# Attention's division put behind the second product, with its reciprocals sent through DRAM as rows, in a two-layer encoder

## The chip, the cores and the metric

The kernel runs on one core of one Trainium2 chip. The metric is the device time of one execution in microseconds; of several runs the median is used. One execution was also recorded by the profiler, and all rows of profile in this document come from such recordings. Engines are named as the profile names them: PE is the tensor engine's matmul unit, PEld its weight load, DVE the vector engine, ACT the scalar engine, POOL the GpSimd engine, SP the engine that issues most transfers.

## The reference

Two transformer layers over 1024 tokens of width 1024, in float32. Layer 0 has two groups of eight heads: A, grouped-query attention with rotary positions, and B, latent attention. Both are dense: every query sees all 1024 keys. Layer 1 has 16 heads that see keys within 128 tokens, with a distance penalty and a learned sink. In all three the output of a head is divided by its sum of exponentials and multiplied by a gate:

```python
# layer 0, group A (B likewise)
p = jax.nn.softmax(sc, axis=-1).astype(v.dtype)
o = jnp.einsum('bkgqs,bskd->bqkgd', p, v)
oa = oa * jax.nn.silu(ga)
# layer 1
p = jnp.exp(sc - m)
denom = jnp.sum(p, axis=-1, keepdims=True) + jnp.exp(sink_l - m)
o = jnp.einsum('bnkgqs,bnskd->bnqkgd', (p / denom).astype(v.dtype), vb)
return (oc * jax.nn.silu(gc)) @ w_out
```

Softmax is the exponentials over their sum. Since the second product (with `v`) is linear, dividing a query's exponentials by their sum gives the same as dividing that query's row of the output, or as dividing its row of the gate.

## The kernel before, in words

Each float32 matrix is split into a high and a low part, and a product is made of two or three matmuls of such parts. Matmuls have 128 x 128 weights and up to 512 columns.

**Layer 0's attention** runs in 32 steps (`run_groups`): head by head, each with two halves of 512 queries. A step makes four score tiles of 128 queries by 1024 keys (`softmax_unit`): PE makes the scores in PSUM, DVE finds each row's maximum (`nm`), ACT makes the exponentials into a tile of SBUF (`Pa` or `Pb` in the profile) and sums them on the way (`sm`), DVE takes the reciprocal (`rs`), and POOL multiplies the tile of 128 x 1024 by it, in place. In the same step PE makes the second product of the step before (`pv_step`): it transposes four 128 x 128 pieces into PSUM, ACT and DVE split them into high and low (`hla`, `hlb`), and two matmuls with `V` add up. In group B two of the eight pieces are split by POOL instead (`pv_ahead`). At the end ACT and DVE move the sum to `og`, 64 partitions for an even head and 64 for an odd one, and POOL multiplies it by the gate (`pv_final`). Two heads share a tile of `og`, which goes to DRAM when both are done (`spill`). Beside this, PE gets matmuls for the gates (`g_step`), and for what group B needs, in the steps of group A.

**Layer 1's attention** runs in 32 steps too: four key heads by eight blocks of 128 queries. `win_S` makes four score tiles of up to 384 keys, DVE adds the penalty, POOL puts the sink into a column behind them, ACT makes the exponentials, DVE takes four reciprocals at once (`dn`), and POOL multiplies each of the four tiles. `win_PV` does the transposes, splits and second product. For three of the four key heads the gate is made after the attention and multiplied into its output `og1` (`g_ft`); for the last the gates (`g1`) are made late and multiplied at the very end (after line 2730). Feature matmuls (`f_step`) fill PE between the steps, with weights that are loaded two tiles ahead and split by POOL (`f_load`).

After each attention comes the output projection (`wino_out`), as seven products of combined blocks, and after layer 1 a last normalisation.

**What sets the order.** No instruction is issued where the code names it. `Recorder` collects all of them; `run` (line 730) plays them through a model of the engines with estimated durations, priorities and limits on buffers, and so puts them into one order. `PLACES` (line 81) then moves single instructions: a pair (i, j) puts i right behind j. `emit` (line 1009) issues the result, so every instruction bears its line 1017 in the profile, and groups are told apart by their tiles. Each engine works through its own instructions in that order, and SP its transfers. `BANKS` gives each PSUM tile its bank. `UA_BUFS` and `SM_BUFS` are the numbers of half tiles (128 x 512) and of small tiles (128 x 16), `RESERVE` what the model keeps free of them.

Of the kernel before, what the change touches and what calls it, by code (L numbers as in the profile page):

```python
# [19 lines left out]
P = 128  # L20
# [20 lines left out]
UA_BUFS = 3  # L41
SM_BUFS = 32
# [3 lines left out]
RESERVE = {"u": 0, "PSUM": 0, "ua": 2, "sm": 11, "SP": 8}  # L46
# [9 lines left out]
AHEAD = {"a": {}, "b": {4: 0, 7: 3}}  # L56
# [983 lines left out]
def encoder_kernel(ctx: ExitStack, tc: tile.TileContext, xt, ada_t, w_c1, w_c2, w_c3, w_g0, w_uq, w_ukv, w_out0, w_v1,  # L1040
# [759 lines left out]

    def softmax_unit(qk, name):
        S = PS(f"S{name}")
        first = None
        for b in range(2):
# [8 lines left out]
        with rec.at(shift=PRIO["exp"]):  # L1815
            nc.scalar.activation(pt, S, AF.Exp, bias=nm[:, 0:1], accum_out=sm[:, 0:1])
# [900 lines left out]
    for g in range(4):  # L2717
        og1[g] = [U(f"og1{g}{half}") for half in range(2)]
        for i in range(NT):
            m0 = m_  # L2720
            if prev is not None:
                m_ = win_PV(*prev)
# [104 lines left out]
```

## Time and profile before

| what | value |
|---|---|
| median of 3 runs | 1132.57 us (1127.54 to 1133.49) |
| profiled execution | 1134.05 us, its span 1132.2 us, mean granted clock 0.985 |
| PE busy | 1102.4 us, 97% of the span |
| DVE, ACT, POOL busy | 978.1, 749.5, 745.3 us |
| layer 0's attention | about 140 to 640 us of the span |
| layer 1's attention | about 770 to 1037 us |

The span runs from the first to the last instruction. A group's row in the profile has the line, the engine, the operation, output and inputs, shapes and count; then busy time and the mean of one in ns; then the engine's idle time just before them, with what ended it. A row of waits has the waiting engine and tile, what it waited for, the total in us, how often, and the longest. A row of the timeline has the start and the length in us. A matmul's end is modelled by the profiler, so a busy PE can still be slower than it could be. The granted clock says at what share of full speed PE was allowed to run.

### The profile page before, as it was taken

What the parts mean: (1) busy time and instruction counts of PE and PEld (TensorE: products, weight loads), DVE (VectorE), ACT (ScalarE), POOL (GpSimd) and SP (SyncE); (2) the same over time, 40 slices, a digit from 0 to 9 for tenths busy, and PEclk for the clock granted to TensorE, in tenths of its full rate; (3) what the DMA queues carried; (4) which work ended last, traced back from release to release, by engine and by line L of the source; (5) the groups of instructions that cost most, each with busy time, mean ns of one, the idle gap of its engine ahead of it and who ended that gap; (6) DMA issues with size and microseconds to landing.
All of it is one profiled execution on the core that took longest, in us unless ns stands there. A gap on an engine that the chain in (4) does not pass through costs nothing.

```text
span 1132.2 us, 17617 instructions
## 1 busy us (share of the span) xinstructions
PE 1102.4 (97%) x5928; PEld 942.9 (83%) x5928; DVE 978.1 (86%) x1604; ACT 749.5 (66%) x1460; POOL 745.3 (66%) x732
## 2 busy tenths in 40 slices
PE   8999999999999999999999999999999999999996
PEld 7898877888887988888888877888888888888785
DVE  5978998898999988887888999998877787778995
ACT  4663554778777877887798742667776776766722
POOL 1135777988986737877879736757675775976422
PEclk7999999999999999999999999999999999999997
DMA  9869863564751486974785477401111221349303
GB/s 368 326 201 318 273 252 78 144 195 125 203 165 15 89 289 207 212 204 160 210 238 191 114 271 245 152 1 38 41 54 56 78 68 42 113 166 336 103 1 149
DMA packets 60026, 183.72 MB, mean 162 GB/s; under 512 B 7200, under 2 KB 9632, under 8 KB 58912
## 3 DMA queue, kind: packets, MB, share of 16 engines
q1 hardware_dynamic: 54464, 159.00, 40.2%
q0 software_dynamic: 4608, 22.02, 10.7%
q10 hardware_dynamic: 864, 1.57, 0.4%
q8 instruction: 47, 0.77, 0.3%
q14 instruction: 43, 0.35, 0.1%
HBM read 147.31 MB, written 70.91 MB: 193 GB/s over the span
## 4 chain that ended last, share of the span: by engine, by line
PE 81%; DVE 12%; issue 2%; ACT 2%; POOL 1%; DMA 1%; POOLq 0%; SPq 0%; DVEq 0%; ACTq 0%
PE psum L1017 81%; DVE nm L1017 1%; DVE xr L1017 1%; DVE hla L1017 1%; DVE t30l L1017 1%; DMA xT<-in_xt 1%; ACT Pb L1017 1%; DVE o L1017 0%; DVE T6l L1017 0%; DVE hlb L1017 0%; DVE s31l L1017 0%; DVE s30l L1017 0%; DVE psum L1017 0%; POOL sq L1017 0%; DVE t40l L1017 0%
## 5 line engine op out<-in xcount | busy, mean ns | idle before, releaser
L1017 DVE TENSOR_REDUCE nm<-psum 128x1 f32<-128x1024 f32 x128 | 155.6, 1219 | 21.0 <-PE psum L1017 18.8
L1017 POOL TENSOR_SCALAR Pa<-Pa,rs 128x1024 f32<-128x1024 f32 x64 | 77.4, 1233 | 34.9 <-DVE rs L1017 30.4
L1017 POOL TENSOR_SCALAR Pb<-Pb,rs 128x1024 f32<-128x1024 f32 x64 | 77.3, 1217 | 32.7 <-DVE rs L1017 29.7
L1017 POOL TENSOR_SCALAR p<-p,dn 128x384 f32<-128x384 f32 (+1 forms) x128 | 69.4, 560 | 33.2 <-DVE dn L1017 32.9
L1017 ACT ACTIVATE Pa<-psum,nm 128x1024 f32<-128x1024 f32 x64 | 71.6, 1119 | 27.6 <-DVE nm L1017 26.0
L1017 DVE TENSOR_TENSOR hla<-psum,hla 128x512 fp32r<-128x512 f32 x128 | 82.6, 683 | 4.4 <-ACT hla L1017 4.2
L1017 ACT ACTIVATE Pb<-psum,nm 128x1024 f32<-128x1024 f32 x64 | 71.9, 1124 | 20.2 <-DVE nm L1017 18.0
L1017 DVE CUSTOM_DVE_ANT_0 p<-psum,relt,sinkn 128x384 f32<-128x384 f32 (+1 forms) x128 | 70.4, 579 | 15.3 <-PE psum L1017 13.8
L1017 PE MATMUL psum<-hla,VA 128*128 128x512 f32 x256 | 80.5, 407 | 1.3 <-DVE og('0', 2)_631 L1017 1.1
L1017 ACT ACTIVATE p<-p,nm 128x385 f32<-128x385 f32 (+1 forms) x128 | 74.8, 591 | 10.2 <-DVE nm L1017 5.6
L1017 ACT CAST hla<-psum 128x512 fp32r<-128x512 f32 x128 | 70.5, 596 | 16.3 <-PE psum L1017 15.3
L1017 PE MATMUL psum<-k,q 128*128 128x512 f32 x256 | 80.5, 401 | 0.6 <-ACT Pb L1017 0.6
L1017 PE MATMUL psum<-hlb,VB 128*128 128x512 f32 x256 | 78.3, 409 | 0.5 <-DVE hlb L1017 0.5
L1017 PE MATMUL psum<-ident,Pa 128*128 128x128 f32 x512 | 73.4, 274 | 0.0
L1017 ACT CAST hl<-psum 128x512 fp32r<-128x512 f32 x88 | 48.7, 590 | 34.2 <-PE psum L1017 30.2
L1017 DVE TENSOR_TENSOR hlb<-psum,hlb 128x512 fp32r<-128x512 f32 x96 | 63.2, 684 | 8.7 <-ACT hlb L1017 8.2
L1017 PE MATMUL psum<-ident,Pb 128*128 128x128 f32 x512 | 70.3, 273 | 0.1
L1017 DVE TENSOR_TENSOR hl<-psum,hl 128x512 fp32r<-128x512 f32 x88 | 57.9, 686 | 12.9 <-ACT hl L1017 10.9
L1017 PEld LDWEIGHTS psum<-ident,Pa 128*128 128x128 f32 x512 | 61.4, 141 | 8.4 <-issue 0.2
L1017 PEld LDWEIGHTS psum<-ident,Pb 128*128 128x128 f32 x512 | 60.3, 140 | 9.0 <-ACT Pb L1017 0.5
L1017 ACT COPY ot<-psum 64x512 f32<-64x512 f32 x64 | 37.4, 584 | 39.6 <-PE psum L1017 38.5
L1017 ACT ACTIVATE sq<-xr 128x512 f32<-128x512 f32 (+2 forms) x30 | 19.3, 658 | 61.3 <-DVE xr L1017 61.3
(1152 smaller groups left out, 3845.3 us busy)
## 6 DMA issues: line engine op xcount, KB each, us to landing
ada<-in_ada_t SPq DMA_DIRECT2D x32, 512.0 KB, 8.1
fs<-in_w_f POOLq DMA_DIRECT2D x12, 768.0 KB, 9.2
adag<-in_ada_t SPq DMA_DIRECT2D x16, 512.0 KB, 5.3
ws<-in_w_out POOLq DMA_DIRECT2D x16, 512.0 KB, 6.5
S<-ws SPq DMA_DIRECT2D x16, 512.0 KB, 4.5
A<-in_w_out SPq DMA_DIRECT2D x12, 512.0 KB, 4.5
o<-spill SPq DMA_DIRECT2D x12, 512.0 KB, 5.5
fs<-in_w_f SPq DMA_DIRECT2D x6, 768.0 KB, 8.9
```

The costliest lines, as they stand in the source:

```text
L1017: fn(*[real(v) for v in a], **{k: real(v) for k, v in kw.items()})
```

## The change

Nothing is divided ahead of the second product. In layer 0 the four sums of a step go into four columns of one small tile, one reciprocal is taken of all four, and SP writes the 512 results to DRAM, one row per head and pair of heads (`keep_sums`). After an odd head the rows of both heads are loaded, each spread over 64 partitions, into a half tile (`rows`). POOL multiplies that tile into the gate (`scale_gate`), and the product of output and gate is made for both heads at once, after the odd head.

In layer 1 the four reciprocals of a block are written to DRAM; after every fourth block two half tiles of rows are loaded. `win_scale` multiplies them into the attention's output, or for the last key head into the late gates.

There are four half tiles instead of three and 12 small tiles instead of 32. `PLACES` is new throughout (5061 pairs for 3541), and `BANKS` from its fourth row on. `pv_ahead` becomes `ahead`, which could serve layer 1 too, but its entry `"1"` is empty.

```diff
-UA_BUFS = 3
-SM_BUFS = 32
+UA_BUFS = 4
+SM_BUFS = 12
-RESERVE = {"u": 0, "PSUM": 0, "ua": 2, "sm": 11, "SP": 8}
+RESERVE = {"u": 0, "PSUM": 0, "ua": 2, "sm": 2, "SP": 8}
-AHEAD = {"a": {}, "b": {4: 0, 7: 3}}
+AHEAD = {"a": {}, "b": {4: 0, 7: 3}, "1": {}}
 PLACES = (
...
-    def softmax_unit(qk, name):
+    def softmax_unit(qk, name, sums):
...
-            nc.scalar.activation(pt, S, AF.Exp, bias=nm[:, 0:1], accum_out=sm[:, 0:1])
+            nc.scalar.activation(pt, S, AF.Exp, bias=nm[:, 0:1], accum_out=sums)
+        return pt
+
+    rs_sp = [dr.tile([2, 1024], F32, name=f"rs_sp{p}") for p in range(8)]
+    rows = {}
+
+    def keep_sums(p, e, half, sums):
+
         r = SM("rs")
-        nc.vector.reciprocal(r[:, 0:1], sm[:, 0:1])
-        nc.gpsimd.tensor_scalar(pt, pt, r[:, 0:1], 1.0, op0=ALU.mult, op1=ALU.mult)
-        return pt
+        nc.vector.reciprocal(r[:, 0:4], sums)
+        nc.sync.dma_start(out=rs_sp[p][e:e + 1, half * 512:(half + 1) * 512].rearrange("o (j q) -> (o q) j", j=4),
+                          in_=r[:, 0:4])
+        if e:
+            c = slice(half * 512, half * 512 + 512)
+            rows[p, half] = UA(f"rows{p}{half}")
+            for e in range(2):
+                load(rows[p, half][e * 64:e * 64 + 64, :], rs_sp[p][e:e + 1, c].partition_broadcast(64)[:, 0])
+
+    def scale_gate(p, half, gate):
+
+        c = slice(half * 512, half * 512 + 512)
+        nc.gpsimd.tensor_tensor(out=gate[:, c], in0=gate[:, c], in1=rows.pop((p, half)), op=ALU.mult)
...
-        nc.gpsimd.tensor_tensor(out=og[r, c], in0=og[r, c], in1=gate[r, c], op=ALU.mult)
+        if h % 2:
+            nc.gpsimd.tensor_tensor(out=og[:, c], in0=og[:, c], in1=gate[:, c], op=ALU.mult)
...
             if g is not None:
+                sums = SM("sm")
                 for j in range(4):
                     with rec.at(at.get(S_AT[j])):
-                        g["P"].append(softmax_unit(g["qk"](j), f"{g['name']}{j}"))
+                        g["P"].append(softmax_unit(g["qk"](j), f"{g['name']}{j}", sums[:, j:j + 1]))
+                keep_sums(g["p"], g["h"] % 2, g["half"], sums[:, 0:4])
             if prev is not None:
+                if prev["h"] % 2:
+                    scale_gate(prev["p"], prev["half"], prev["gate"]())
...
         nc.vector.reciprocal(dn[:, 8:12], dn[:, 0:4])
-        for j in range(4):
-            pt = Ps[j // 2][:, (j % 2) * 512:(j % 2) * 512 + n * P]
-            nc.gpsimd.tensor_scalar(pt, pt, dn[:, 8 + j:9 + j], 1.0, op0=ALU.mult, op1=ALU.mult)
+        half = i // 4
+        nc.sync.dma_start(out=rs1_sp[g][half].rearrange("j (i q) -> q i j", i=4)[:, i % 4], in_=dn[:, 8:12])
+        if i % 4 == 3:
+            for a in range(2):
+                rows1[g, half, a] = UA(f"rows1{g}{half}{a}")
+                for e in range(2):
+                    load(rows1[g, half, a][e * 64:e * 64 + 64, :],
+                         rs1_sp[g][half, 2 * a + e:2 * a + e + 1].partition_broadcast(64)[:, 0])
         return Ps, lo, n
+
+    def win_scale(g, half):
+
+        o = (og1[g] if g < 3 else g1)[half]
+        for a in range(2):
+            c = slice(a * 512, a * 512 + 512)
+            nc.gpsimd.tensor_tensor(out=o[:, c], in0=o[:, c], in1=rows1.pop((g, half, a)), op=ALU.mult)
...
                 m_ = win_PV(*prev)
+                if prev[0] < 3 and prev[1] % 4 == 3:
+                    win_scale(prev[0], prev[1] // 4)
...
     for half in range(2):
+        win_scale(3, half)
         o = keep[half, 3] = og1[3][half]
```

More of the change, by code (lines that the diff above doesn't have):

```diff
@@ L81 @@
 PLACES = (
[437 rows of a table removed]
[626 rows of a table added]
 )
 BANKS = (
-    "0231501627345101206260125476354215032732341504104052666030223154145666667777012310404243521022454040",
-    "7723230160404761106042534242017116767236242444515132526264623156720620532234670146060345554267201606",
-    "0224465746606025467016706042307635475312406004513203025327311431646467431647525603016417124640226745",
-    "3016460202364713460453534022406064073141050625626250462476720627245664350620724601005132462517574714",
-    "2606047553220201071567442424610135722462040122351624623570231124614646616347523402424673365702402663",
-    "7137004043032657144604502642716312043014461561531032110615615315372047605103642424632574633617527721",
-    "6525561332646320426152450715266206512672451611626455365427704230234740255723001231253351421423621426",
-    "6471124545745172704534700772007442126172402167574251212344724205771607205121044204476104676237210612",
-    "34316025402301054701012365354737034201370112401227016270342701333120621001",
+    "0231501627345101206260125476353215042732341504104052666030223154145666667777012310404243521022454040",
+    "7723230160404761106042534242017116767236242444515132526264526135720620532234670146060345554267201606",
+    "0224465746606025467016706042307635475312406004513203025127311431646467431647525603016437124640226745",
+    "3016460223762013460453542032306064073151054625626257462006420621140244350626724101065132462516554014",
+    "2757045663220201067517642421100615472462130230026446423570330124614646125364423462420673165462402673",
+    "6776004043436257104604472604156312043014461561731032110615617315372645607103642424632574633617525721",
+    "6525561332646320426152450715266206512672451611626455365427704230234740255723001231253371421423621426",
+    "6451124545745772704534700312007442126172402167574251212344724205771607206121544204470154056237215012",
+    "34317025402301074701012365354737034201370112401227016270342701333120621001",
 )
@@ L1813, in softmax_unit, with ahead @@
         pt = U(f"P{name}")
-        sm = SM("sm")
         with rec.at(shift=PRIO["exp"]):
-            nc.scalar.activation(pt, S, AF.Exp, bias=nm[:, 0:1], accum_out=sm[:, 0:1])
-        r = SM("rs")
-        nc.vector.reciprocal(r[:, 0:1], sm[:, 0:1])
-        nc.gpsimd.tensor_scalar(pt, pt, r[:, 0:1], 1.0, op0=ALU.mult, op1=ALU.mult)
-        return pt
-    def pv_ahead(Ps, kt, name):
-        pt = PT(f"T{name}{kt}")
-        transposes(lambda j: pt[:, j * P:(j + 1) * P], [Ps[j][:, kt * P:(kt + 1) * P] for j in range(4)], T_LAST)
-        hl = UR(f"hl{name}{kt}")
-        t = UA(f"t{name}{kt}")
+            nc.scalar.activation(pt, S, AF.Exp, bias=nm[:, 0:1], accum_out=sums)
[3 more added lines that the diff above has]
+    def keep_sums(p, e, half, sums):
+        r = SM("rs")
+        nc.vector.reciprocal(r[:, 0:4], sums)
[9 more added lines that the diff above has]
+        nc.gpsimd.tensor_tensor(out=gate[:, c], in0=gate[:, c], in1=rows.pop((p, half)), op=ALU.mult)
+    def ahead(parts, last_, name):
+        pt = PT(f"T{name}")
+        transposes(lambda j: pt[:, j * P:(j + 1) * P], parts, last_)
+        hl = UR(f"hl{name}")
+        t = UA(f"t{name}")
         nc.scalar.copy(t, pt)
@@ L1870, in run_groups @@
                         if slow[k2] == kt:
-                            early[k2] = pv_ahead(prev["P"], k2, prev["name"])
+                            early[k2] = ahead([p_[:, k2 * P:(k2 + 1) * P] for p_ in prev["P"]], T_LAST,
+                                              f"{prev['name']}{k2}")
                     last[n - 1, kt] = pv_step(prev["P"], prev["V"](kt), acc, kt, prev["name"], early.get(kt))
             if g is not None:
+                sums = SM("sm")
                 for j in range(4):
                     with rec.at(at.get(S_AT[j])):
-                        g["P"].append(softmax_unit(g["qk"](j), f"{g['name']}{j}"))
+                        g["P"].append(softmax_unit(g["qk"](j), f"{g['name']}{j}", sums[:, j:j + 1]))
+                keep_sums(g["p"], g["h"] % 2, g["half"], sums[:, 0:4])
             if prev is not None:
+                if prev["h"] % 2:
+                    scale_gate(prev["p"], prev["half"], prev["gate"]())
                 with rec.at(shift=PRIO["fin"]):
@@ L1947, in encoder_kernel @@
             groupsA.append(dict(
-                name=f"a{h}{half}", h=h, half=half, qk=qk_of,
+                name=f"a{h}{half}", h=h, half=half, p=h // 2, qk=qk_of,
                 V=lambda kt, g=g: VA[kt // 4][:, kt % 4, g, :, :].rearrange("p s d -> p (s d)"),
@@ L2114, in encoder_kernel @@
             groupsB.append(dict(
-                name=f"b{h}{half}", h=h, half=half, qk=qk_of,
+                name=f"b{h}{half}", h=h, half=half, p=4 + h // 2, qk=qk_of,
                 V=lambda kt, h=h: VB[h // 4, kt // 2][:, kt % 2, h % 4, :, :].rearrange("p s d -> p (s d)"),
@@ L2613, in encoder_kernel @@
     g_done = {}
+    rows1 = {}
+    rs1_sp = [dr.tile([2, 4, 512], F32, name=f"rs1_sp{g}") for g in range(4)]
     def g_ft(p):
@@ L2662, in win_S @@
         nc.vector.reciprocal(dn[:, 8:12], dn[:, 0:4])
-        for j in range(4):
-            pt = Ps[j // 2][:, (j % 2) * 512:(j % 2) * 512 + n * P]
-            nc.gpsimd.tensor_scalar(pt, pt, dn[:, 8 + j:9 + j], 1.0, op0=ALU.mult, op1=ALU.mult)
-        return Ps, lo, n
+        half = i // 4
[6 more added lines that the diff above has]
+                         rs1_sp[g][half, 2 * a + e:2 * a + e + 1].partition_broadcast(64)[:, 0])
+        return Ps, lo, n
+    def win_scale(g, half):
[3 more added lines that the diff above has]
+            nc.gpsimd.tensor_tensor(out=o[:, c], in0=o[:, c], in1=rows1.pop((g, half, a)), op=ALU.mult)
     def win_PV(g, i, Ps, lo, n, og):
         acc = PV(f"pv1_{g}{i}")
+        early = {}
         for t in range(n):
             kt = lo + t
-            pt = PT(f"T1_{g}{i}{t}")
-            transposes(lambda j: pt[:, j * P:(j + 1) * P],
-                       [Ps[j // 2][:, (j % 2) * 512 + t * P:(j % 2) * 512 + t * P + P] for j in range(4)], T1_LAST)
-            hl = UR(f"hl1_{g}{i}{t}")
-            with rec.at(shift=PRIO["hi1"]):
-                nc.scalar.copy(hl[:, 0:512], pt)
-            with rec.at(shift=PRIO["lo1"]):
-                sub(hl[:, 512:1024], pt, f(hl[:, 0:512]))
+            parts = lambda t_: [Ps[j // 2][:, (j % 2) * 512 + t_ * P:(j % 2) * 512 + t_ * P + P] for j in range(4)]
+            for t2 in AHEAD["1"]:
+                if AHEAD["1"][t2] == t:
+                    early[t2] = ahead(parts(t2), T1_LAST, f"1_{g}{i}{t2}")
+            hl = early.get(t)
+            if hl is None:
+                pt = PT(f"T1_{g}{i}{t}")
+                transposes(lambda j: pt[:, j * P:(j + 1) * P], parts(t), T1_LAST)
+                hl = UR(f"hl1_{g}{i}{t}")
+                with rec.at(shift=PRIO["hi1"]):
+                    nc.scalar.copy(hl[:, 0:512], pt)
+                with rec.at(shift=PRIO["lo1"]):
+                    sub(hl[:, 512:1024], pt, f(hl[:, 0:512]))
             V = V1[kt // 2][:, kt % 2, g].rearrange("p s d -> p (s d)")
```

1063 rows, old and new, of the table PLACES are left out of this document.

## The prediction, as it was put on record

> **What bounds the kernel now.** I read the page's head first, then busy time by stage, then who makes TensorE wait.
>
> ```profile
> span 1132.2 us, 17617 instructions
> ...
> PE 1102.4 (97%) x5928; PEld 942.9 (83%) x5928; DVE 978.1 (86%) x1604; ACT 749.5 (66%) x1460; POOL 745.3 (66%) x732
> ```
>
> TensorE (PE) is busy for 97% of the span: 1132.2 − 1102.4 = 29.8 us is all the idle time there is. The stages show where it lies (length, then busy us of PE, weight loads, DVE, ACT and POOL, then granted clock, DMA share, GB/s). Layer 0's attention runs from about 140 to 640 us, layer 1's from 770 to 1037.
>
> ```profile
> 140.00:250.00 110.00, 105.97 (x542) 88.46 (x541) 98.14 (x129) 69.49 (x120) 88.34 (x73) 0.98 0.53 158
> 250.00:440.00 190.00, 186.85 (x1068) 157.68 (x1067) 176.98 (x289) 145.42 (x274) 139.98 (x147) 0.99 0.55 164
> 440.00:660.00 220.00, 218.88 (x1199) 184.22 (x1198) 194.07 (x283) 177.45 (x314) 173.71 (x148) 1.00 0.68 188
> 660.00:760.00 100.00, 94.98 (x515) 81.19 (x515) 97.51 (x117) 46.24 (x71) 58.59 (x31) 1.00 0.52 169
> 760.00:1040.00 280.00, 280.00 (x1474) 240.12 (x1473) 222.09 (x535) 199.75 (x473) 195.59 (x260) 1.00 0.27 94
> 1040.00:1132.20 92.20, 80.30 (x392) 67.78 (x390) 76.45 (x93) 39.30 (x59) 32.03 (x21) 0.92 0.27 97
> 160.00:180.00 20.00, 17.23 (x82) 14.16 (x81) 16.97 (x15) 8.20 (x13) 15.99 (x8) 0.98 0.54 149
> 180.00:200.00 20.00, 20.00 (x93) 16.53 (x93) 15.59 (x23) 11.77 (x22) 14.61 (x13) 0.94 0.29 88
> 340.00:360.00 20.00, 17.86 (x86) 14.38 (x87) 18.70 (x31) 11.99 (x22) 10.06 (x8) 0.91 0.04 7
> ```
>
> The reader should see three things. Layer 1's attention has no PE idle at all (280.00 of 280), so relief for POOL can save nothing there. Layer 0's attention has 4.03 + 3.15 + 1.12 = 8.3 us. And two places lose clock as well: 0.98 and 0.94 over 160 to 200 us, 0.91 over 340 to 360. A share missing from the clock is time lost: (0.02 + 0.06) × 20 = 1.6 us and 0.09 × 20 = 1.8 us. The waits of PE that fall into layer 0's attention:
>
> ```profile
> PE psum L1017 <- DVE gk L1017: 2.8, 1, 2.8
> ...
> PE psum L1017 <- DVE gT L1017: 1.3, 2, 1.0
> ...
> PE psum L1017 <- DVE hla L1017: 1.2, 1, 1.2
> PE psum L1017 <- DVE og('0', 2)_631 L1017: 1.1, 1, 1.1
> ...
> PE psum L1017 <- ACT Pb L1017: 0.6, 1, 0.6
> PE psum L1017 <- ACT Pa L1017: 0.6, 1, 0.6
> PE psum L1017 <- DVE hlb L1017: 0.5, 1, 0.5
> ```
>
> None names POOL, the engine that divides. The transposes that read the divided tiles hardly ever wait:
>
> ```profile
> L1017 PE MATMUL psum<-ident,Pa 128*128 128x128 f32 x512 | 73.4, 274 | 0.0
> L1017 PE MATMUL psum<-ident,Pb 128*128 128x128 f32 x512 | 70.3, 273 | 0.1
> ```
>
> So the division's own latency (exponential, reciprocal, multiplication, transpose) is hidden. What the change can save is indirect: DVE is the engine PE waits for, and POOL's work stretches DVE's. The clearest case stands just ahead of the waits for og and hla:
>
> ```profile
> 332.87 3.34 POOL L1017 TENSOR_SCALAR Pa<-Pa,rs 128x1024 f32<-128x1024 f32 x3 [1.46 <-ACT hla L1017]
> ...
> 336.73 1.06 POOL L1017 TENSOR_SCALAR wuqh<-wuqs 128x768 fp32r<-128x768 f32 x1
> 337.53 1.26 POOL L1017 TENSOR_SCALAR ckvTh<-lat 128x1024 fp32r<-128x1024 f32 x1
> 338.55 1.25 POOL L1017 TENSOR_SCALAR cqTh<-lat 128x1024 fp32r<-128x1024 f32 x1
> ```
>
> ```profile
> 332.28 0.28 DVE L1017 TENSOR_TENSOR krt<-ropeb 128x128 f32<-128x128 f32 x1
> ...
> 336.44 3.64 DVE L1017 TENSOR_TENSOR krt<-krt 128x256 f32<-128x256 f32 x1
> 340.11 0.68 DVE L1017 TENSOR_TENSOR og('0', 2)_631<-psum,ot 64x512 f32<-64x512 f32 x1
> ```
>
> DVE's addition of 256 columns takes 3.64 us, where one of 128 took 0.28. It ends when POOL's three weight splits end (338.55 + 1.25 = 339.80). Those splits stood behind three divisions (3.34 us). og and PE come after it.
>
> **The change part by part.** Removed from POOL are all divisions; from DVE, most reciprocals.
>
> ```profile
> L1017 POOL TENSOR_SCALAR Pa<-Pa,rs 128x1024 f32<-128x1024 f32 x64 | 77.4, 1233 | 34.9 <-DVE rs L1017 30.4
> L1017 POOL TENSOR_SCALAR Pb<-Pb,rs 128x1024 f32<-128x1024 f32 x64 | 77.3, 1217 | 32.7 <-DVE rs L1017 29.7
> L1017 POOL TENSOR_SCALAR p<-p,dn 128x384 f32<-128x384 f32 (+1 forms) x128 | 69.4, 560 | 33.2 <-DVE dn L1017 32.9
> ...
> L1017 POOL TENSOR_TENSOR og<-og,g 128x512 f32<-128x512 f32 x16 | 22.4, 1407 | 7.1 <-DVE g L1017 4.4 <-DVE og L1017 2.5
> ...
> L1017 POOL TENSOR_TENSOR og('0', 4)_904<-og('0', 4)_904,gB 64x512 f32<-64x512 f32 x4 | 5.1, 1287 | 1.1 <-DVE og('0', 4)_904 L1017 1.0
> ```
>
> ```profile
> L1017 DVE RECIPROCAL rs<-sm 128x1 f32<-128x1 f32 x128 | 17.7, 154 | 8.3 <-ACT Pb L1017 3.9 <-ACT Pa L1017 3.7
> ...
> L1017 DVE RECIPROCAL dn<-dn 128x4 f32<-128x4 f32 x32 | 5.6, 174 | 10.0 <-ACT p L1017 9.8
> ```
>
> POOL loses 77.4 + 77.3 + 69.4 = 224 us. It gains 16 multiplications of gates by rows in layer 0 and 16 in layer 1, 32 × 1.407 = 45 us. The 32 half-height products of output and gate (1.287 each, 41 us) become 16 of full height (16 × 1.407 = 23 us). Net: 224 − 45 + 18 = 197 us less. On DVE, 128 reciprocals of 0.154 become 32 of 0.174: 17.7 − 5.6 = 12 us less, and about three quarters of the 8.3 us that stood before them. Neither sum is on the path; they count where DVE is late.
>
> *The krt case.* With no divisions ahead of them the splits can start some 3.3 us sooner, and the addition at 336.44 runs free. I take back all of it: 1.1 + 1.2 idle and 1.8 of clock, 4.1 us. Bounds: 0 (another order lets the two meet again) and 4.1.
>
> *The gk case.* PE waits 2.8 us at 178.6 and loses 1.6 in clock: 4.4 us. Just ahead, a split on DVE was stretched:
>
> ```profile
> 173.85 3.39 DVE L1017 TENSOR_TENSOR G4l<-hf,G4h 128x1024 fp32r<-128x1024 f32 x1
> ```
>
> POOL worked on weight splits at that time, which remain, with one division among them. I take half, 2.2; bounds 0 and 4.4.
>
> *The other waits.* 1.3 + 0.6 + 0.6 + 0.5 = 3.0 us. DVE and ACT are relieved only a little; half, 1.5; bounds 0 and 3.0.
>
> The page "TensorE: Matmul & The Clock Gate" of the Trainium skill (HAM oscillation) gives the rule that PE gaps up to about 3.4 us don't throttle. This trace differs: the longest wait above was 2.8 us and the clock fell to 0.94 right after it. By that rule the two cases would be worth their idle alone, 2.3 and 1.4 in place of 4.1 and 2.2, and the time would be about 1128.5; the trace decides.
>
> **What it adds on the queues.** 64 small writes of reciprocals to DRAM (512 numbers of 4 bytes each), and 64 loads that spread one row over 64 partitions (128 KB), all on SP. No such write is in the trace. Rows nearest, issue to landing:
>
> ```profile
> q<-qr_sp SPq DMA_DIRECT2D x16, 128.0 KB, 4.5
> ...
> spill<-og SPq DMA_DIRECT2D x6, 512.0 KB, 3.0
> ```
>
> ```profile
> SPq L1017 <- PE psum L1017: 391.8, 82, 57.5
> ```
>
> For the load I take 4.5 us, the row of the same size. For the write the bounds are 3.0 us (the quickest row, far more bytes) and twice the load, 9.0, for 512 separate elements; I take 4.5. Rows are then there 9 us after the reciprocal, 13.5 at worst. Layer 0 has 32 steps in 500 us, 15.6 us each, and its rows are used a step later: hidden on either bound. Layer 1 has 32 steps in 280 us, 8.75 each, so its rows come about 0.3 us late, at worst 4.8. SP's queue blocks on each load until its write has landed, and the loads of weights and the moves of keys and queries behind it wait too; but SP itself spends 391.8 us waiting for PE's progress, so I cost this at nothing. Without that cover each block would cost the write's 4.5 us to whoever waits for a weight.
>
> On POOL, a multiplication that waits for late rows holds up the weight splits and the sink columns behind it, and ACT's exponentials wait for the latter. At 0.3 us I cost it at 0; the other bound is a rival below.
>
> *The tail.* The last gates get one more multiplication, 1.4 us, ahead of their product with the output.
>
> ```profile
> 1053.88 1.31 POOL L1017 TENSOR_TENSOR og<-og,g 128x512 f32<-128x512 f32 x1 [3.50 <-DVE g L1017]
> ```
>
> ```profile
> 1057.08 0.68 DVE L1017 TENSOR_TENSOR o<-o,og 128x512 f32<-128x512 f32 x1
> ```
>
> The product ends at 1055.19 and its reader starts at 1057.08, after other DVE work: 1.9 us of cover for 1.4. I take 0; without the cover, 1.4.
>
> *Buffers and order.* A fourth half-tile pays for the rows held over a step; 12 small tiles instead of 32 serve a kernel that uses six per step of layer 0 where it used twelve. I take 0 for both. The list that reorders instructions is new throughout, not only around the attention. It can lose a wait elsewhere or win one: I add one new wait of 1.1 us, the mean size of those listed, with bounds from −5.0 (all idle of 660 to 760 us gone) to +5.0 (as much again).
>
> **Sum.** −4.1 − 2.2 − 1.5 + 0 + 1.1 = −6.7 us. The profiled execution took 1134.05 us (1.85 around its span), so 1127.4 in its terms. It lies 1.5 us over the median of the runs shown, 1132.57; in terms of that median the forecast is 1126 us, 0.6% faster.
>
> **Rivals.**
>
> *Nothing to win.* PE is full, the division never stood on its path, and the collisions of DVE and POOL come back at other places. For: no PE wait names POOL, and the weight splits remain. Against: 197 us less to collide with. 0 to −3 us: about 1131.
>
> *The order wins beyond the attention.* Everything in layer 0's attention goes (4.1 + 4.4 + 3.0 = 11.5) and the 5.0 of 660 to 760 as well: 1132.57 − 16.5 = 1116. For: the order changes everywhere. Against: in 660 to 760 DVE is busy for 97.51 of 100 us and gets no relief.
>
> *Rows late in layer 1 (slower).* One mechanism, at POOL's in-order queue: rows that land after 8.75 us block it at seven of the eight half-ends (the last is in the tail). At the worst bound 4.8 × 7 = 34 us of POOL; if half of that reaches PE through the exponentials, 17 us: 1126 + 17 = 1143. It decides from landings of about 11 us on; there 2.3 × 7 / 2 = 8 us eat the gain. Against: POOL is idle for 84 of 280 us there, and less busy after. The Trainium skill's "DMA: Bandwidth & Descriptors" (Rules for kernel authors) says that a strided last dimension becomes one descriptor per element and should be made contiguous instead; these writes do what it warns of, and no run here shows their price.
>
> *It doesn't do what it says:* not possible, since the removed instructions are gone from the code.
>
> **How the numbers follow.** About 0.5% (5.7 us) is what a measurement of this kernel can tell from no change, so faster means below 1126.9 and slower above 1138.2. Forecast 0.43, and since it lies close to that limit I give 0.28 of it to faster and 0.15 to the same; larger win 0.18, all faster; nothing to win 0.25, the same; late rows 0.14, of which 0.12 slower and 0.02 the same. Faster 0.46, same 0.42, slower 0.12. The forecast's own range, from its terms' bounds, is 1120 to 1133 (all of 11.5 gained with one new wait, or nothing gained). The range over the cases is 1115 to 1139: the larger win at its end, and late rows up to a third of their worst price.
>
> **What would show it.** Right: POOL's busy time near 548 us; no DVE addition stretched over 3 us ahead of an og; no clock below 1.00 near 180 and 345 us; PE idle in 140 to 660 us down from 8.3 to about 3. Wrong: POOL waiting for rows (a DMA named before its multiplications) and PE busy below 280 in layer 1's attention; or new PE waits for DVE of 1 to 3 us with clock lost behind them; or a PE span as before with the idle moved.

## The result, and the profile after

The changed kernel takes 1319.99 us (median of 4 runs, 1316.02 to 1323.66) against 1131.69 (median of 4, 1127.54 to 1133.49): 1.167 times as long, 95% interval 1.162 to 1.172. The forecast of 1126 us was wrong by 194 us and in its sign.

The head of the page after, and the packets that it counts:

```profile
span 1321.2 us, 17433 instructions
...
PE 1151.5 (87%) x5928; PEld 966.5 (73%) x5928; DVE 961.8 (73%) x1508; ACT 751.2 (57%) x1460; POOL 540.7 (41%) x492
...
DMA packets 98937, 192.23 MB, mean 145 GB/s; under 512 B 42016, under 2 KB 44448, under 8 KB 97824
```

PE does the same 5928 matmuls and stands idle for 169.7 us instead of 29.8. POOL's 540.7 us are close to what the prediction worked out (548). Packets under 512 bytes number 42016; the kernel before had 7200, and the kernel below that leaves out the 64 writes has 8224. Busy time by stage shows where the idle time lies; layer 0's group A is the first two rows, its group B the third, layer 1's attention the fourth:

```profile
140.00:250.00 110.00, 103.82 (x532) 86.57 (x531) 91.25 (x108) 67.97 (x118) 54.35 (x45) 0.97 0.59 146
250.00:440.00 190.00, 179.85 (x1022) 150.44 (x1020) 163.40 (x240) 139.24 (x261) 87.06 (x98) 0.99 0.73 149
440.00:755.00 315.00, 251.22 (x1241) 204.97 (x1242) 198.98 (x254) 182.61 (x323) 103.88 (x94) 0.89 0.73 156
860.00:1215.00 355.00, 296.54 (x1454) 245.74 (x1453) 219.95 (x525) 196.89 (x469) 138.30 (x144) 0.91 0.49 75
```

Group B takes 315 us where it took 220, layer 1's attention 355 where it took 280, both with a granted clock near 0.9 where it was 1.00. That is 95 and 75 us of the whole loss of 188, as near as stages with round limits can tell. Who waits in SP's queue (`SPq`) and on POOL:

```profile
SPq L1206 <- DMA rs_sp<-rs: 237.2, 25, 15.8
SPq L1206 <- PE psum L1206: 160.9, 53, 15.3
...
SPq L1206 <- DMA rs_sp<-dn: 79.5, 10, 11.7
```

```profile
POOL gT L1206 <- DMA rows<-rs_sp: 72.3, 6, 27.3
POOL gB L1206 <- DMA rows<-rs_sp: 44.4, 5, 11.8
...
POOL og L1206 <- DMA rows<-rs_sp: 31.9, 6, 11.2
...
POOL g L1206 <- DMA rows<-rs_sp: 11.5, 1, 11.5
```

SP now waits 316.7 us, 35 times, for a write of reciprocals to land, 9.0 us each on the mean. It had waited 391.8 us for PE's progress; 160.9 are left. POOL waits 160.1 us for rows; the gates `gT` and `gB` are layer 0's, `og` and `g` layer 1's. One stretch of layer 1 shows how that reaches PE. SP's transfers first, then POOL, ACT and PE, all in order of time:

```profile
924.83 1.37 SPq L1206 DMA_DIRECT2D wf12s<-fs  x2
926.29 0.39 SPq L1206 DMA_DIRECT2D rs_sp<-dn  x1
938.55 1.09 SPq L1206 DMA_DIRECT2D rows<-rs_sp  x2
...
942.07 0.50 SPq L1206 DMA_DIRECT2D wf13s<-in_w_f  x1
```

```profile
936.48 1.05 POOL L1206 TENSOR_SCALAR wf12h<-wf12s 128x1024 fp32r<-128x1024 f32 x1 [9.34 <-DMA wf12s<-fs]
...
947.84 1.26 POOL L1206 TENSOR_TENSOR og<-og,rows 128x512 f32<-128x512 f32 x1 [4.15 <-DMA rows<-rs_sp]
951.77 1.04 POOL L1206 TENSOR_SCALAR wf13h<-wf13s 128x1024 fp32r<-128x1024 f32 x1 [2.67 <-DMA wf13s<-in_w_f]
952.78 0.19 POOL L1206 TENSOR_SCALAR p<-sinkn 128x2 f32<-128x2 f32 x1
```

```profile
953.01 0.62 ACT L1206 ACTIVATE p<-p,nm 128x385 f32<-128x385 f32 x1 [7.32 <-POOL p L1206]
```

```profile
955.95 1.52 PE L1206 MATMUL psum<-hl,V 128*128 128x512 f32 x2 [8.33 <-ACT hl L1206]
```

The write issued at 926.29 lets the rows behind it go at 938.55, 12.3 us later. POOL then waits for rows and for a weight, the sink column comes at 952.78, ACT's exponentials wait 7.32 us for it, and PE waits 8.33 for a cast that stands behind them. But a second thing is seen at the top: the weight `wf12s` was issued before that write, at 924.83, and POOL still waited until 936.48 for it. Nothing in the order of SP's queue explains that.

### The profile page after: what moved, and what is told of

Its sections match the earlier page's. It is cut to its first block, busy times and chain, and to the rows that moved or that the text cites. A ratio compares the mean times of both kernels' runs of the same rounds, so it can differ in the third digit from the quotient of the medians.

```text
span 1321.2 us, 17433 instructions
## 1 busy us (share of the span) xinstructions
PE 1151.5 (87%) x5928; PEld 966.5 (73%) x5928; DVE 961.8 (73%) x1508; ACT 751.2 (57%) x1460; POOL 540.7 (41%) x492
## 2 busy tenths in 40 slices
DMA packets 98937, 192.23 MB, mean 145 GB/s; under 512 B 42016, under 2 KB 44448, under 8 KB 97824
## 5 line engine op out<-in xcount | busy, mean ns | idle before, releaser
L1206 PE MATMUL psum<-hlb,VB 128*128 128x512 f32 x256 | 88.8, 442 | 32.1 <-ACT hlb L1206 16.8
L1206 PE MATMUL psum<-k,q 128*128 128x512 f32 x256 | 87.9, 432 | 25.0 <-DMA q<-qnp 15.9
L1206 DVE TENSOR_TENSOR hla<-psum,hla 128x512 fp32r<-128x512 f32 x128 | 83.4, 683 | 16.8 <-ACT hla L1206 16.5
L1206 ACT ACTIVATE Pa<-psum,nm 128x1024 f32<-128x1024 f32 x64 | 71.5, 1118 | 35.2 <-DVE nm L1206 21.9
L1206 PE MATMUL psum<-hl,V 128*128 128x512 f32 x176 | 64.3, 428 | 26.1 <-ACT hl L1206 22.4
L1206 PEld LDWEIGHTS psum<-hlb,VB 128*128 128x128 f32 x256 | 49.9, 205 | 46.0 <-ACT hlb L1206 18.0
L1206 PEld LDWEIGHTS psum<-k,q 128*128 128x128 f32 x256 | 51.3, 208 | 37.9 <-issue 8.6
L1206 ACT CAST hlb<-psum 128x512 fp32r<-128x512 f32 x96 | 53.2, 599 | 30.4 <-DMA q<-qnp 18.9
## 6 DMA issues: line engine op xcount, KB each, us to landing
ws<-in_w_out POOLq DMA_DIRECT2D x16, 512.0 KB, 11.8
```

The costliest lines, as they stand in the source:

```text
L1206: fn(*[real(v) for v in a], **{k: real(v) for k, v in kw.items()})
```

## The experiments

Four theories were put first. A: SP's in-order queue stands still while a load of rows waits for its write to land. B: the writes of 4-byte pieces slow other transfers themselves. C: the new order of issue is bad. D: POOL waits for rows (the prediction's slower rival). Later E: SP's wait for the reciprocal itself. A piece is a run of bytes that lie side by side in DRAM and are written from one place. The times below are medians: of two runs for the kernels above 1150 us, of six to twelve for the others; the two kernels with isolated writes ran once, and of them only the writes are read.

### Loads that don't wait for the writes, and no writes

```diff
-load(rows[...], <the row just written>)
+load(rows[...], <a row of a constant table>)      # rows_from_input, all 64 loads
+w.call = lambda *a, **kw: None                     # writes_left_out: also no write
```

> The changed kernel, with all 64 writes of reciprocals still issued at their places, but the 64 loads spread a row of a constant input table instead of the row just written. So no load waits for a write's landing. The output is left undivided by the sums. Theory A (SP's in-order queue stands still while a load waits for its write to land, and the weights, keys and queries behind it come late): nearly all of the 188 us goes, 1130 to 1180 us, and SP's waits for rs_sp (about 450 us together after the change) become small. Theory B (the 4-byte packets slow the other transfers in the DMA engines themselves): the time stays at 1260 us or above. Theory C (the new order of issue is bad): stays at 1260 or above. Theory D (POOL's queue waits for rows): POOL's waits for rows go and the time falls by about their 116 us, to some 1200.

> As with the rows from the constant table, and the 64 writes of reciprocals are left out as well, so the output is again undivided by the sums; every other instruction stands in the changed kernel's order. Theories A, B and D: 1120 to 1140 us, since no 4-byte packet and no wait for one is left; what this kernel saves on the one that still writes is the share of B. Theory C: 1200 us or above.

Measured: 1255.22 us with the writes (1.109 times before, 1.102 to 1.117), 1127.29 without (0.995, 0.993 to 0.997; the kernel before, run alongside, 1131.89). No range was hit: A's ended at 1180, B's and C's began at 1260. C falls: the new order without the writes is faster than before. Loads that wait for the writes' data, on SP (A) and POOL (D) together, explain 64.8 of the 188 us; writes whose data nobody reads cost the other 128 us, and that is B's side. The two are not cleanly parted, for SP still waits 44.4 us for such writes to land:

```profile
SPq L1206 <- DMA rs_sp<-rs: 27.1, 10, 7.7
...
SPq L1206 <- DMA rs_sp<-dn: 17.3, 6, 6.0
```

In each of these 16 waits the trace has SP waiting for the semaphore (the counter that tells of a landing) that the next transfer in its queue uses itself. So that transfer wants the semaphore, not the data. The loads of rows land after 11.8 us beside the writes and 4.4 without them, by the median from issue to landing:

```profile
rows<-in_tabs_d SPq DMA_DIRECT2D x64, 128.0 KB, 11.8
```

```profile
rows<-in_tabs_d SPq DMA_DIRECT2D x64, 128.0 KB, 4.4
```

D's 116 us don't fit: POOL's waits for rows fell by only 71.5 us, from the 160.1 of the four rows above to 88.6 (38.9, 25.8, 16.5 and 7.4), and the time by about as much, but the other 128 us remained when none of the written rows was read.

### The kernel before, with layer 1's writes added

```diff
 nc.vector.reciprocal(dn[:, 8:12], dn[:, 0:4])
+nc.sync.dma_start(out=<unread DRAM, 4-byte pieces>, in_=dn[:, 8:12])
```

> The kernel before, and after each of layer 1's 32 reciprocals SP writes the same 512 numbers in 4-byte pieces to DRAM, where nobody reads them. It computes the whole reference. Theory A: SP waits only for the reciprocal and not for the landing, so 1130 to 1145 us. Theory B: layer 1's attention loses what it lost in the changed kernel, 75 us, some 1200 us. Theories C and D: 1130 to 1140 us.

Measured: 1266.65 us (1.119, 1.115 to 1.124). The 32 writes alone cost 135 us with the old order and with all divisions in place. SP waits only 3.4 us, twice, for them to land, so A has no part in this. From 780 to 1160 us, most of the stage that holds the writes, PE is idle for 95.7 us and its clock is down to 0.86:

```profile
780.00:1160.00 380.00, 284.27 (x1328) 235.94 (x1327) 195.90 (x480) 179.21 (x430) 173.07 (x239) 0.86 0.48 54
```

It is more than B's 75. SP now waited 221.8 us for reciprocals in an order that was not made for it, so this kernel's excess is not the writes' alone.

### The same writes with fewer pieces

```diff
-out=<512 places>, in_=r[:, 0:4]
+out=<256 places>, in_=r[:, 0:2]        # half_pieces
+out=<one place of 16 bytes>, in_=r[0:1, 0:4]   # one_piece
```

> As with the rows from the constant table (output undivided by the sums), and each of the 64 writes carries one piece of 16 bytes from one partition instead of 512 pieces of 4. Every transfer is issued where it was, and SP still waits for each reciprocal. Theory B (the pieces slow the other transfers): about 1127 us, as with the writes left out. Theory E (SP's in-order wait for the reciprocal itself makes what is behind it late): near the 1255 us of the kernel with 512 pieces, 1230 at least.

> As the one before, with 256 pieces of 4 bytes in each write instead of 512 or 1. If the loss goes by the number of pieces: half of 128 us, 1180 to 1200. If there is cover that is used up first: well below, 1135 to 1160. If each write costs the same: 1255.

Measured: 1125.61 us with one piece (0.995, 0.993 to 0.997; before 1131.59), 1224.63 with 256. E falls for this order: with every wait for a reciprocal in place nothing is lost. But half the pieces keep 99 of 130 us (1224.63 − 1125.61 against 1255.22 − 1125.61). All three expectations for 256 pieces were missed; the price is neither by the piece nor by the write.

### The writes from another queue

```diff
-nc.sync.dma_start(out=<row>, in_=r[:, 0:4])
+nc.scalar.dma_start(out=<row>, in_=r[:, 0:4])
```

> Rows from the constant table (output undivided by the sums), the 64 writes with all their 512 pieces, but issued by ACT instead of SP, so that they stand in another queue than the loads; ACT waits for each reciprocal for that. If the pieces hold up only what stands behind them in their own queue: 1130 to 1160 us, and the rows' loads land in about 4.4 us as without the writes. If they slow the DMA engines for every queue: 1230 or above, loads near 11.8 us.

Measured: 1274.11 us (1.126, 1.123 to 1.130). The loads on SP land after 9.3 us, between the two cases. Another queue doesn't free the transfers of SP's queue, and the time is no better than from SP (1255.22). This run alone doesn't say how they are held: SP waits 109.2 us, 22 times, for these writes to land, again for semaphores that its own next transfers use. ACT also waits for the reciprocals here, so the 19 us more are not told apart.

### The same numbers in longer pieces

```diff
-rs_sp[p][...].rearrange("o (j q) -> (o q) j", j=4)    # 512 pieces of 4 bytes
+rs_sp[p][...].rearrange("o (q j) -> (o q) j", j=4)    # 128 of 16; layer 1: 256 of 8
```

> The changed kernel with the same numbers written in longer pieces: layer 0's 32 writes as 128 pieces of 16 bytes instead of 512 of 4, layer 1's first 24 writes as 256 pieces of 8 bytes; the multiplication by the row reads it with the matching stride. The whole reference is computed. If the number of pieces sets the landing (A or B): layer 0's half of the loss goes nearly whole and layer 1's by half, 1180 to 1230 us. If each write costs the same whatever its pieces: 1300 us or above. The strided multiplication may cost POOL up to twice its 1.4 us, which is off the path.

Measured: 1156.79 us (1.022, 1.018 to 1.026), better than the 1180 to 1230 expected. Here 256 pieces of 8 bytes in most of layer 1, with all waits for landings in place, cost far less than 256 of 4 did without them. So the size or the place of the pieces matters, and not their number alone.

### The disputed cost by itself

Writes of several shapes, alone, behind the end of the kernel before; a small load behind each waits for its landing, so the time from a write's issue to that load's issue is the landing. Then one load of 128 KB behind a write.

```diff
+write(d, ...); nc.sync.dma_start(out=got[0:1, 0:1], in_=d[0:1, 0:1])   # three times each
```

> The kernel before, full reference, and behind its end, one after the other and with nothing else running, writes to DRAM of eight shapes, each followed on SP by a small load that waits for its landing: 1 piece of 16 bytes, 16 of 128, 128 of 16, 256 of 8, 256 of 4, 512 of 4 (as in the change), 512 of 4 set 512 bytes apart, 512 of 512 bytes. Then a load of 128 KB (one row to 64 partitions) behind one piece, behind 512 pieces of 4 bytes from SP's queue, from ACT's queue, and behind 16 pieces of 128. If the price goes by the number of pieces: landings rise with it, some 2 to 3 us for 1 and 16 pieces and 8 to 12 for 512 of any size. If pieces that share a stretch of DRAM are what costs: 512 pieces set apart land in half the time of 512 beside each other. If the engines are held for every queue: the load behind ACT's write lands as late as behind SP's, 5 us or more later than behind one piece; if only the own queue, ACT's costs nothing.

Median of three (us):

| write | landing |
|---|---|
| 1 piece of 16 bytes | 1.2 |
| 16 of 128 bytes | 1.4 |
| 128 of 16 bytes, side by side | 1.6 |
| 256 of 8 bytes, side by side | 3.1 |
| 256 of 4 bytes, side by side | 8.5 |
| 512 of 4 bytes, side by side (the change's) | 8.8 |
| 512 of 4 bytes, 512 bytes apart | 2.6 |
| 512 of 512 bytes | 2.3 |

Two of these in the timeline, 512 pieces side by side (`w512x` from 1143.95) and the same number set apart (`a512x`):

```profile
1143.95 0.38 SPq L2749 DMA_DIRECT2D w512x<-src  x1
...
1151.75 0.21 SPq L2751 DMA_DIRECT2D got<-w512x  x1
1152.01 0.38 SPq L2749 DMA_DIRECT2D a512x<-src  x1
...
1155.30 0.21 SPq L2751 DMA_DIRECT2D got<-a512x  x1
```

Busy time, DMA share and GB/s (the last two columns) while `w512x` was under way:

```profile
1143.95:1145.50 1.55, 0.00 (x0) 0.00 (x0) 0.10 (x1) 0.00 (x0) 0.00 (x0) 0.50 0.16 1
1145.50:1151.70 6.20, 0.00 (x0) 0.00 (x0) 0.18 (x2) 0.00 (x0) 0.00 (x0) 0.50 0.00 0
```

Its packets are through in 1.6 us; for 6.2 more nothing moves, and then it has landed. The number of pieces is not the price: 512 of them, with 128 times the bytes or far apart, land in 2.3 to 2.6 us. 256 or 512 pieces of 4 bytes beside each other take 8.5 and 8.8.

The load of 128 KB landed 2.9, 2.9 and 2.8 us after its issue behind one piece; 8.2, 9.6 and 8.2 behind 512 pieces side by side from SP; 8.1, 3.0 and 5.9 beside the same from ACT, which issued its write about 0.3 us after the load; 3.0, 2.9 and 3.1 behind 16 pieces. One of the second kind, and the same columns before and during its wait:

```profile
1227.89 0.38 SPq L2749 DMA_DIRECT2D bsp<-src  x1
1228.32 0.51 SPq L2778 DMA_DIRECT2D got<-in_tabs_d  x1
...
1236.56 0.17 DVE L2779 COPY got<-got 64x16 f32<-64x16 f32 x1 [8.70 <-DMA got<-in_tabs_d]
```

```profile
1228.30:1231.00 2.70, 0.00 (x0) 0.00 (x0) 0.00 (x0) 0.00 (x0) 0.00 (x0) 0.50 0.32 49
1231.00:1236.50 5.50, 0.00 (x0) 0.00 (x0) 0.00 (x0) 0.00 (x0) 0.00 (x0) 0.50 0.00 0
```

All packets, the load's too (49 GB/s for 2.7 us are its 128 KB), are through by 1231. Then nothing moves for 5.5 us, and only then is the load told to have landed. The section "Queues, rings and completion order" of the Trainium skill's "DMA: Bandwidth & Descriptors" has a rule that fits: a transfer's completion signal is an ordered write, and lands only after every earlier write of that DMA engine, in whichever queue. By it a load waits for the slowest write ahead of it on its engines; the 0 GB/s above agree, and so do two of the three loads beside ACT's writes (8.1 and 5.9 us). The third landed after 3.0, and no run shows why. The rule says what a slow write holds up, not why the write is slow.

### The same number of pieces, set apart, in the kernel

```diff
-w: 512 pieces of 4 bytes side by side (rows from the constant table)
+apart = dr.tile([512, 128], F32); out=apart.rearrange("(j q) c -> q j c", j=4)[:, :, 0]
```

> As with the rows from the constant table (output undivided by the sums), and each of the 64 writes still carries 512 pieces of 4 bytes, issued by SP at its place, but each piece goes to a place of its own, 512 bytes from the next, where nobody reads it. If the number of pieces is the cause: 1255 us as before. If it is that neighbouring pieces of 4 bytes share a stretch of DRAM (the isolated writes landed after 8.6 us side by side, 2.6 us apart): 1125 to 1140 us.

Measured: 1125.50 us (0.995, 0.993 to 0.997; before 1131.25). This settles the cause: 64 writes of 512 pieces of 4 bytes at their places cost nothing where the pieces don't neighbour, and 130 us where they do, with the same 42016 packets under 512 bytes. SP's waits for such a landing are gone too, so the 130 us are B with what the 44.4 us of waits above cost; that B alone is enough was seen in the kernel before with writes added.

### How far apart

> The kernel before, full reference, and behind its end isolated writes of 512 pieces of 4 bytes at distances of 4, 8, 16, 32, 64, 128, 256 and 512 bytes, then 64, 128 and 256 pieces side by side. If pieces that share a stretch of DRAM wait for one another, the landing falls from about 8.6 us to 2.6 as the distance grows, and the distance at which it has fallen shows the stretch: by what was measured (8-byte pieces side by side 3.3 us, 16-byte ones 1.7), between 16 and 64 bytes. With the number of pieces side by side it rises little: 256 were 8.4 us.

512 pieces of 4 bytes, median of three: 9.0 us at a distance of 4 bytes, 3.2 at 8, 2.8 at 16, 2.0 at 32, and 1.9 to 2.0 from 64 to 512. Side by side, 64 pieces already take 6.1 us, 128 take 6.3, 256 take 7.5. The distances of 4 and 32 bytes (`bya`, `byd`) and the 64 pieces (`nx`):

```profile
1172.64 0.38 SPq L2749 DMA_DIRECT2D bya<-src  x1
1180.63 0.21 SPq L2751 DMA_DIRECT2D got<-bya  x1
...
1187.46 0.38 SPq L2749 DMA_DIRECT2D byd<-src  x1
1189.41 0.21 SPq L2751 DMA_DIRECT2D got<-byd  x1
...
1198.82 0.33 SPq L2749 DMA_DIRECT2D nx<-src  x1
1204.96 0.21 SPq L2751 DMA_DIRECT2D got<-nx  x1
```

As expected the landing has fallen at 32 bytes; the largest step is from 4 to 8. That 256 pieces cost nearly as much as 512 fits half the pieces' keeping three quarters of the loss. Why neighbouring pieces land so late is not seen in a trace; it stays open.

### The change with its writes mended

```diff
 tc.nc.vector.reciprocal(x[:, <4 columns of 8 or 16>], i)
+tc.nc.vector.transpose(y, x)             # 32x32 blocks, once in 2 or 4 reciprocals
-one write of 512 pieces of 4 bytes
+for b in range(4): nc.sync.dma_start(out=out[b], in_=y[32*b:32*b+n, :])   # n pieces of 128 bytes
```

> The changed kernel, full reference: DVE turns the reciprocals in blocks of 32 by 32 first (8 columns of layer 0's two reciprocals, 16 of layer 1's four), so that each four writes carry 32 or 64 pieces of 128 bytes instead of 1024 or 2048 of 4; 128 writes in all. Layer 1's distances are loaded after layer 0, since their space is borrowed. If the number of pieces was the cause: 1125 to 1135 us, near the 1127.3 without any write, and a version that is as fast as the kernel before or faster. If waiting for landings of any size costs (theory A alone): 1150 or above.

Measured: 1138.40 us (1.007, 1.005 to 1.009; before 1131.59), short of the 1125 to 1135 expected. The writes were 96 in all, not 128. 182 us are back, but one wait of PE was new: 7.46 us for a move of queries. SP's queue shows why, a load of rows right ahead of it standing from 460.82 (end of the writes) to 464.96:

```profile
458.57 2.25 SPq L2010 DMA_DIRECT2D rs_sp<-relt  x4
464.96 0.47 SPq L2023 DMA_DIRECT2D rows<-rs_sp  x1
465.52 1.19 SPq L1206 DMA_DIRECT2D q<-qnp  x2
```

```profile
473.39 1.65 PE L1206 MATMUL psum<-k,q 128*128 128x512 f32 x3 [7.46 <-DMA q<-qnp]
```

```diff
-a load of rows that comes up before its write: issued right behind the write (14 of layer 0's 32 loads)
+the same load: at the place of the pair's second load, here behind the queries' moves
```

> The version with reciprocals turned by DVE, full reference, but both loads of a pair of rows are issued at the place of the second one, instead of directly behind the write. In the version before it PE had one wait of 7.5 us, for a move of queries that stood in SP's queue behind such a load. Theory A (the load that waits for its write's landing holds up what is behind it): that wait goes and the clock lost behind it, 1125 to 1130 us. If the 13 us have another cause: 1136 to 1140.

Measured: 1129.09 us (before 1132.40; ratio 0.9984, 0.9967 to 1.0001), within what A gave. The wait is gone (PE is busy for 220.00 of 220 us from 440 to 660), and 9.3 us with it. Only the loads' places differ, so this is A alone, most of it at this place. This kernel computes what the reference does; by its interval it is at best 0.3% faster than the kernel before, and at worst the same.

## Why the prediction was wrong, point by point

*What bounds the kernel, and the gain: right.* With harmless writes (set apart) the time is 1125.5 us, 0.5% under before, where 1126 was forecast. The stages of that kernel, and the places that the prediction named:

```profile
140.00:250.00 110.00, 109.50 (x567) 91.92 (x566) 96.22 (x117) 72.34 (x127) 59.42 (x51) 1.00 0.55 170
250.00:440.00 190.00, 187.72 (x1090) 159.11 (x1089) 174.26 (x255) 147.66 (x277) 87.12 (x99) 1.00 0.67 173
440.00:660.00 220.00, 220.00 (x1201) 186.33 (x1200) 188.57 (x247) 175.63 (x307) 106.92 (x91) 1.00 0.77 213
160.00:180.00 20.00, 20.00 (x98) 16.62 (x97) 15.12 (x13) 10.49 (x18) 12.32 (x8) 1.00 0.53 164
180.00:200.00 20.00, 20.00 (x104) 16.76 (x103) 18.08 (x26) 12.68 (x23) 15.65 (x19) 1.00 0.62 176
340.00:360.00 20.00, 19.99 (x120) 16.66 (x119) 19.69 (x29) 15.81 (x30) 10.36 (x10) 1.00 0.54 171
```

PE's idle time from 140 to 660 us is 0.50 + 2.28 + 0 = 2.8 us; about 3 was said. *The krt case* came as priced: no clock is lost near 345 us, and in that kernel's timeline the addition takes 0.42 us, not 3.64.

```profile
332.03 0.42 DVE L1206 TENSOR_TENSOR krt<-krt 128x256 f32<-128x256 f32 x1
```

*The gk case* was taken at half and came whole: 20.00 of 20 us busy from 160 to 180 us and from 180 to 200, at a clock of 1.00. The sum is small, as forecast, and in part by luck: gk gave 2.2 us more than was taken, and against it stand 1.1 us of PE idle in layer 1's attention (278.89 busy of 280) and 2.4 more after 1040 us (14.3, where it was 11.9). That kernel's rows hold constants, not reciprocals, and the full version with mended writes keeps about half of it (3.3 us of 5.8, between the medians, with an interval that reaches no gain). One end of the forecast's range doesn't follow from its terms: all 11.5 us gained and one new wait of 1.1 give 1122, not 1120.

*"What it adds on the queues": wrong.* Three steps failed; the second holds most of the loss.

1. "SP itself spends 391.8 us waiting for PE's progress, so I cost this at nothing." The total of a wait over the whole kernel was taken for cover at each place. SP's waits for landings came to 316.7 us, PE's cover shrank to 160.9, and 64.8 us reached the end (1319.99 against 1255.22, where no load waits for the written data). That holds POOL's waits for rows too, and SP still waited 44.4 us in the second kernel, so 64.8 is the size of this step only roughly. The sentence behind it had the right form, "each block would cost the write's 4.5 us to whoever waits for a weight"; a wait was 9.0.

2. The write was priced by its own data only. A landing of 4.5 us was taken, with 9.0 as the upper bound; the bound nearly held for a write alone (7.8 to 10.0 in six isolated ones) and not in the kernel (12.3 in the stretch above; medians of 10.9 and 9.9 where the loads read the table). But the sum has no term at all for the transfers beside it, and there is most of the loss: 1255.22 − 1125.50 = 129.7 us, from writes whose data nobody reads. The load was taken at 4.5 and is 4.4 beside harmless writes, 11.8 beside these.

3. "Hidden on either bound", of layer 0's rows. POOL waited 72.3 + 44.4 = 116.7 us for them, up to 27.3 at once, and group B lost more time (95 us) than layer 1's attention (75). The sum of write and load was put at 9 to 13.5 us. With the landings measured beside these writes, 10.9 and 11.8 us, it would be 22.7, more than the 15.6 of a step.

The first two make up the loss: 64.8 + 129.7 − 6.2 (the gain, 1131.69 − 1125.50) = 188.3. These are steps from kernel to kernel, so they add up by themselves; the third is a part of them.

*The rival "rows late in layer 1 (slower)": its mechanism was seen, its price was not.* The stretch at 947 us shows it step by step: rows late, POOL held, sink column late, exponentials late, PE idle. POOL's waits for rows, 160.1 us in the four rows above, can't be parted from A by these runs: both fell in the kernel with rows from the table. The rival looked at layer 1's half-ends only, gave 1143, and held landings up to 9.0. For layer 1 its worst bound, 34 us of POOL at seven half-ends, was not far off: 31.9 + 11.5 = 43.4 us in seven waits. The sign that the prediction named for it came too: POOL waits for rows, and PE is busy for 296.54 of 355 us in layer 1's attention.

*The rule that the prediction weighed against the change* (the Trainium skill's "DMA: Bandwidth & Descriptors", Rules for kernel authors: a strided last dimension becomes one descriptor per element; make it contiguous) pointed the right way, and was left with a chance of 0.14. The number of elements is not what cost here: 512 elements of their own land in 2.0 us when they lie 32 bytes apart.

*Tail, buffers, order:* with harmless writes the kernel is 0.5% faster with them in. The 2.4 us more of PE idle after 1040 us may be the tail's 1.4 in part; no run parts the three.

## What to carry to other kernels

Price an added transfer twice, once for whoever reads its data and once for every other transfer in flight, and look for both in a run with the transfer kept and its reader taken away. A queue's total of waiting is no cover: what counts is what stands behind the blocked entry at that place. Taking the reader away doesn't take all waits away, so read the queue's waits again afterwards. Small results go to DRAM in few long pieces; here a turn in blocks of 32 by 32 on DVE and the loads put behind the moves that PE needs first gave back 191 of the 194 us between 1319.99 and 1125.50.

## What the runs showed of the hardware

Pieces of 4 bytes written side by side to DRAM land after 6.1 us (64 pieces) to 9.0 us (512), against 2.0 us for 512 pieces 32 bytes or more apart. The packets of the write of 512 pieces shown above were through within 1.6 us of its issue; the rest of the time the engines moved nothing (0 GB/s), and other transfers are held all the same: a load of 128 KB that lands in 2.9 us behind a write of one piece takes 8.2 to 9.6 behind 512 pieces side by side, and 8.1, 3.0 and 5.9 if these came from ACT's queue. The section "Issuing engines are not separate DMA queues" of the Trainium skill's "DMA: Bandwidth & Descriptors" says that all queues end on the same 16 engines; the two loads that ACT's writes held (8.1 and 5.9 us) agree.
